# Row means from summed weight columns, so that centring starts before the last product

## The chip, the cores and the metric

The kernel runs on one core of a Trainium2 chip. The metric is device time in microseconds (us) for one execution. All times below come from one profiled execution or from the timed runs of the kernel before.

## The reference, cut to what matters

One decoder layer: a projection of `x` (256 rows of 1024), two attention branches, gates, an output projection and a layer norm over the 1024 columns of a row. Only the end is touched:

```python
merged = gate_a * ya + gate_b * yb
out = jnp.einsum('bsd,de->bse', merged, w_out[l])
x = layer_norm(DN_ALPHA * x + out, ln_gamma[l], ln_beta[l])

def layer_norm(x, g, b):
    mu = jnp.mean(xf, axis=-1, keepdims=True)
    var = jnp.mean(jnp.square(xf - mu), axis=-1, keepdims=True)
    return (xf - mu) * lax.rsqrt(var + LN_EPS) * g + b
```

## The kernel before

Each float32 weight tile (`wraw`, 128x1024) is loaded on the SP queue, rounded on ScalarE to `wh` and its remainder is formed on VectorE as `wl`, so that three products (`mh*wh`, `ml*wh`, `mh*wl`) stand for one float32 product. `fetch` issues the load and the rounding, `split` the remainder; both run several tiles ahead of TensorE. The order of instructions on each engine is the order in which the code is written.

The end of the program is a loop over two blocks of 128 rows (`t`). For each block, `products` multiplies the eight 128-deep slices of the merged activations (`mm`, its halves `mh` and `ml`) by the eight tiles of `w_out`, 24 products for each group of columns. Block 0 runs all 1024 columns at once in two PSUM banks of tag `acc`. Block 1 runs three groups one after the other: columns 0 to 512, 512 to 768 (the third quarter) and 768 to 1024 (the last quarter), in banks of tag `sc`. After each group VectorE adds the residual (line 373) and takes the statistics of each quarter (line 375, `bn_stats`).

When the last quarter of a block has its statistics, line 383 joins them to mean and variance, ScalarE takes the root (385) and the norm is applied in three pieces. Columns 0 to 416 and 416 to 832 get two VectorE passes each: `centre` (390: subtract the mean, times gamma) and 404 (times 1/deviation, plus beta), then a store on the SP queue. Columns 832 to 1024 go over ScalarE (398: scale and `shift`, a small VectorE result of line 397), then two GpSimd passes (399: times gamma, 400: plus beta) and a store on the ACT queue (406). Block 0's norm runs beside block 1's products; nothing runs beside block 1's.

Of the kernel before, what the change touches and what calls it, by code (L numbers as in the profile page):

```python
# [11 lines left out]
F32 = mybir.dt.float32  # L12
F32R = mybir.dt.float32r
# [4 lines left out]
P = 128  # L18
# [18 lines left out]

WARM = 9
RAWS = 5


@with_exitstack
def hybrid_layer(ctx: ExitStack, tc: tile.TileContext, xT, x2, w_t, w_v, w_a, w_b, w_o,
# [56 lines left out]
    order += [("o", k) for k in range(NK)]  # L100
    ahead = {"v": 2, "t": 3, "a": 4, "b": 5, "o": 7}
    raws, ready = {}, {}

    def fetch(kind, n):
# [12 lines left out]
        src = {"v": lambda: w_v[:, n, :], "t": lambda: w_t[n], "a": lambda: w_a[n], "b": lambda: w_b[n],  # L117
               "o": lambda: w_o[n * P:(n + 1) * P, :]}[kind]()
        raw = wp.tile([P, 1024], F32, tag="raw", name="wraw", bufs=RAWS)
        wh = wp.tile([P, 1024], F32R, tag="wh", name="wh", bufs=8)  # L120
        parts = 2 if (kind, n) == ("v", 0) else 1
        cuts = [slice(i * width // parts, (i + 1) * width // parts) for i in range(parts)]
        for cut in cuts:
            nc.sync.dma_start(raw[:, cut], src[:, cut])
        for cut in cuts:
            nc.scalar.activation(wh[:, cut], raw[:, cut], AF.Copy)  # L126
        raws[kind, n] = raw, wh, width

    def split(kind, n):
# [6 lines left out]
        wl = wp.tile([P, 1024], F32R, tag="wl", name="wl", bufs=8)  # L136
        nc.vector.tensor_sub(wl[:, :width], raw[:, :width], wh[:, :width].bitcast(F32))  # L137
        ready[kind, n] = wh, wl

    cursors = [0, 0]  # L140
# [216 lines left out]
    nc.sync.dma_start(gb[:, 1, :], beta.to_broadcast([P, D]))  # L357
    sd = work.tile([P, 1], F32, name="sd")
    nc.scalar.activation(sd, eps, AF.Sqrt)
    for t in range(2):  # L360
        ts = slice(t * P, (t + 1) * P)
        res = work.tile([P, D], F32, tag="res", name="res")
        st = work.tile([P, 4, 6], F32, name="st")

        def products(cuts):
            accs = [bank("acc" if t == 0 else "sc" if i < 2 else "pt")[:, :b - a] for i, (a, b) in enumerate(cuts)]
            for k in range(NK):
                wh, wl = weights("o", k)
                for a, w, s0, s1 in ((mh, wh, k == 0, False), (ml, wh, False, False), (mh, wl, False, k == NK - 1)):
                    for acc, (lo, hi) in zip(accs, cuts):  # L370
                        nc.tensor.matmul(acc, a[:, k, ts], w[:, lo:hi], start=s0, stop=s1)  # L371
            for acc, (lo, hi) in zip(accs, cuts):
                nc.vector.scalar_tensor_tensor(res[:, lo:hi], xr[:, t, lo:hi], ALPHA, acc, op0=ALU.mult, op1=ALU.add)
                for q in range(lo // S, hi // S):
                    nc.vector.bn_stats(st[:, q, :], res[:, q * S:(q + 1) * S])

        if t == 0:
            products([(0, 512), (512, 1024)])
        else:
            for cut in ((0, 512), (512, 768), (768, 1024)):  # L380
                products([cut])
        mv = work.tile([P, 2], F32, name="mv")
        nc.vector.bn_aggr(mv, st)  # L383
        sd = work.tile([P, 1], F32, name="sd")
        nc.scalar.activation(sd, mv[:, 1:2], AF.Sqrt, bias=eps)  # L385
        cuts = [slice(0, 416), slice(416, 832)]
        last = slice(832, D)

        def centre(cut):
            nc.vector.scalar_tensor_tensor(res[:, cut], res[:, cut], mv[:, 0:1], gb[:, 0, cut],  # L390
                                           op0=ALU.subtract, op1=ALU.mult)

        centre(cuts[0])
        rstd = work.tile([P, 1], F32, name="rstd")
# [6 lines left out]
        for cut in cuts:  # L401
# [76 lines left out]
```

## Time and profile before

| | us |
|---|---|
| median of 3 timed runs | 203.61 (203.3 to 203.8) |
| the profiled execution | 203.97 |
| its span, first to last instruction | 202.2 |
| the difference, outside the span | 1.77 |
| TensorE busy | 192.9 of 202.2 |
| VectorE busy | 134.2 |
| ScalarE busy | 113.2 |
| GpSimd busy | 17.1 |

The span is what the trace shows; the device time has 1.77 us more in this execution. "Busy" counts the time in which an instruction of the engine was under way. TensorE's granted clock had a mean of 0.994 of full speed.

### The profile page before, as it was taken

Reading aid. Unit: us, or ns where it says so; the run is one execution under the profiler, and the core shown is the slowest. Engines: PE = TensorE matmul, PEld = TensorE weight load, DVE = VectorE, ACT = ScalarE, POOL = GpSimd, SP = SyncE. Lnnn points to the kernel's source line nnn. Section 1 sums busy time; section 2 is a strip of 40 time slices with the busy share of each in tenths; the row PEclk is TensorE's granted clock in tenths of the full one; section 3 lists DMA queues with packets and bytes.
Section 4 is the critical chain, followed back from the end, with each engine's and each line's share of the span. In section 5 each row is a group of like instructions: output and inputs, shape, how many; then the busy total and the mean of one; then the engine's idle time right before and its main releaser. Section 6 shows DMA issues by size and latency. Waiting matters only on the chain.

```text
span 202.2 us, 3837 instructions
## 1 busy us (share of the span) xinstructions
PE 192.9 (95%) x1469; PEld 181.7 (90%) x1469; DVE 134.2 (66%) x268; ACT 113.2 (56%) x225; POOL 17.1 (8%) x29
## 2 busy tenths in 40 slices
PE   8899999999999999999999999999999999999940
PEld 3699999999998998989999999999999999888940
DVE  0595268999987874685777546446585867557753
ACT  4585648677985776775679444246554636620110
POOL 7070000110110100100000000000000000000303
PEclk9999999999999999999999999999999999999997
DMA  5999999947354233054667865474737499200202
GB/s 129 318 393 334 256 295 302 282 132 246 120 172 143 105 104 109 6 177 139 199 203 230 296 209 169 146 216 135 289 143 258 133 349 362 96 2 0 104 0 104
DMA packets 14081, 37.42 MB, mean 185 GB/s; under 512 B 1632, under 2 KB 5744, under 8 KB 14064
## 3 DMA queue, kind: packets, MB, share of 16 engines
q1 hardware_dynamic: 13520, 36.51, 55.8%
q0 software_dynamic: 256, 0.49, 0.7%
q8 instruction: 11, 0.18, 0.4%
q10 hardware_dynamic: 288, 0.20, 0.3%
q14 instruction: 6, 0.05, 0.1%
HBM read 35.75 MB, written 1.44 MB: 184 GB/s over the span
## 4 chain that ended last, share of the span: by engine, by line
PE 93%; DMA 2%; DVE 1%; ACT 1%; POOL 0%; POOLq 0%; SPq 0%; issue 0%
PE ps_acc L165 21%; PE ps_acc L166 21%; PE ps_acc L168 21%; PE ps_sc L371 6%; PE ps_acc L371 5%; PE ps_acc L277 4%; PE ps_sc L277 3%; PE ps_pt L242 3%; PE ps_o L259 2%; DMA wraw<-in_w_v 2%; PE ps_sc L205 1%; PE ps_sc L206 1%; PE ps_sc L207 1%; PE ps_o L261 1%; POOL res L399 0%; POOLq L474 0%
## 5 line engine op out<-in xcount | busy, mean ns | idle before, releaser
L137 DVE TENSOR_TENSOR wl<-wraw,wh 128x1024 fp32r<-128x1024 f32 (+1 forms) x61 | 70.2, 1167 | 7.8 <-ACT wh L126 7.5
L165 PE MATMUL ps_acc<-xh,wh 128*128 128x256 f32 x296 | 72.8, 284 | 0.0
L166 PE MATMUL ps_acc<-xl,wh 128*128 128x256 f32 x296 | 72.6, 283 | 0.0
L126 ACT ACTIVATE wh<-wraw 128x1024 fp32r<-128x1024 f32 (+2 forms) x62 | 60.8, 995 | 9.8 <-DMA wraw<-in_w_t 5.4
L165 PEld LDWEIGHTS ps_acc<-xh,wh 128*128 128x128 f32 x296 | 56.8, 192 | 0.5 <-issue 0.2
L166 PEld LDWEIGHTS ps_acc<-xl,wh 128*128 128x128 f32 x296 | 56.8, 192 | 0.3
L168 PE MATMUL ps_acc<-xh,wl 128*128 128x256 f32 x296 | 41.5, 283 | 0.0
L168 PEld LDWEIGHTS ps_acc<-xh,wl 128*128 128x128 f32 x296 | 38.2, 192 | 0.0
L339 ACT ACTIVATE sg<-ps_acc,bg 128x256 f32<-128x256 f32 x16 | 7.6, 475 | 20.9 <-PE ps_acc L168 20.9
L166 PE MATMUL ps_acc<-yl,wh 128*128 128x256 f32 x64 | 16.1, 283 | 0.0
L165 PE MATMUL ps_acc<-yh,wh 128*128 128x256 f32 x64 | 16.1, 283 | 0.0
L344 DVE TENSOR_TENSOR ga<-ps_acc,sg 128x256 f32<-128x256 f32 x8 | 3.4, 423 | 14.7 <-ACT wh L126 14.7
L165 PEld LDWEIGHTS ps_acc<-yh,wh 128*128 128x128 f32 x64 | 12.3, 192 | 0.0
L166 PEld LDWEIGHTS ps_acc<-yl,wh 128*128 128x128 f32 x64 | 12.3, 192 | 0.0
L399 POOL TENSOR_TENSOR res<-res,gb 128x192 f32<-128x192 f32 x2 | 1.8, 916 | 109.9 <-ACT res L398 109.9
L371 PE MATMUL ps_sc<-wh,mm 128*128 128x256 f32 (+1 forms) x48 | 10.7, 318 | 0.0
L168 PE MATMUL ps_acc<-yh,wl 128*128 128x256 f32 x64 | 10.3, 283 | 0.0
L349 ACT ACTIVATE mm<-m 128x256 fp32r<-128x256 f32 x8 | 3.3, 417 | 11.4 <-DVE m L348 11.4
L385 ACT ACTIVATE sd<-mv,eps 128x1 f32<-128x1 f32 x2 | 0.6, 294 | 16.1 <-DVE mv L383 16.1
L168 PEld LDWEIGHTS ps_acc<-yh,wl 128*128 128x128 f32 x64 | 8.8, 192 | 0.0
L371 PEld LDWEIGHTS ps_sc<-wh,mm 128*128 128x128 f32 x48 | 8.1, 191 | 0.7
L371 PE MATMUL ps_acc<-wh,mm 128*128 128x512 f32 x32 | 8.6, 390 | 0.0
(142 smaller groups left out, 269.0 us busy)
## 6 DMA issues: line engine op xcount, KB each, us to landing
wraw<-in_w_t SPq DMA_DIRECT2D x37, 512.0 KB, 3.7
wraw<-in_w_o SPq DMA_DIRECT2D x8, 512.0 KB, 4.6
wraw<-in_w_v SPq DMA_DIRECT2D x7, 320.0 KB, 5.1
toep<-rd SPq DMA_DIRECT2D x16, 128.0 KB, 7.3
wraw<-in_w_a SPq DMA_DIRECT2D x4, 512.0 KB, 3.8
wraw<-in_w_b SPq DMA_DIRECT2D x4, 512.0 KB, 4.3
xraw<-in_xT SPq DMA_DIRECT2D x8, 128.0 KB, 5.0
xr<-in_x SPq DMA_DIRECT2D x1, 1024.0 KB, 8.1
```

The lines of the kernel that those rows point to most:

```text
L126: nc.scalar.activation(wh[:, cut], raw[:, cut], AF.Copy)
L137: nc.vector.tensor_sub(wl[:, :width], raw[:, :width], wh[:, :width].bitcast(F32))
L165: nc.tensor.matmul(acc, wh[:, cols[k]], ah[:, a0 + k, :], start=(k == 0), stop=False)
L166: nc.tensor.matmul(acc, wh[:, cols[k]], al[:, a0 + k, :], start=False, stop=False)
L168: nc.tensor.matmul(acc, wl[:, cols[k]], ah[:, a0 + k, :], start=False, stop=(k == n - 1))
L242: nc.tensor.transpose(pt[:, b * P:(b + 1) * P], pr[:, j, b * P:(b + 1) * P], ident)
L259: nc.tensor.matmul(o[r, :], vv[:, 0, c], pts[:, :S], start=True, stop=False)
L277: nc.tensor.matmul(vacc[t][c], a[:, k, t * P:(t + 1) * P], w[:, c * 320:(c + 1) * 320], start=s0, stop=s1)
L339: nc.scalar.activation(sg, acc, AF.Sigmoid, bias=bg[:, at:at + 1])
L344: nc.vector.tensor_mul(ga[:, c, :], acc, sg)
L349: nc.scalar.activation(mh[:, c, :], m, AF.Copy)
L371: nc.tensor.matmul(acc, a[:, k, ts], w[:, lo:hi], start=s0, stop=s1)
```

## The change

The tiles `wh` and `wl` are laid out as four quarters of 258 columns (`OW`) in place of one stretch of 1024, so that each quarter has two spare columns. For the tiles of `w_out`, ScalarE and VectorE write through that layout, and VectorE also sums the last quarter of each weight tile over its columns into one column of `sums`. After block 0's products are issued, `place_sums` splits these sums into a rounded part and a remainder, and GpSimd copies them into the two spare columns of the third quarter: 16 copies of 128x2. In block 1 the third quarter's products run over 258 columns, so that column 256 of its bank holds what the last quarter's products will add up to along the row. With the statistics of three quarters and a sum of the residual's last quarter (`xs`) this gives minus the mean (`below`) one quarter earlier. Columns 0 to 768 of block 1 are centred and multiplied by gamma in the time of the last quarter's products. The pieces change too: columns 0 to 192 (`early`) now go over ScalarE and GpSimd, 192 to 640 and 640 to 1024 over VectorE.

```diff
-        wh = wp.tile([P, 1024], F32R, tag="wh", name="wh", bufs=8)
+        wh = wp.tile([P, 4 * OW], F32R, tag="wh", name="wh", bufs=8)
...
+            nc.vector.tensor_reduce(sums[:, n:n + 1], raw[:, 3 * S:], axis=mybir.AxisListType.X, op=ALU.add)
...
+    xs = work.tile([P, 1], F32, name="xs")
+    nc.vector.tensor_reduce(xs, xr[:, 1, 3 * S:], axis=mybir.AxisListType.X, op=ALU.add)
+    nc.vector.tensor_scalar_mul(xs, xs, -ALPHA / D)
+    def place_sums():
+        parts = [work.tile([P, NK], F32R, name=f"sums_{i}", bufs=1) for i in range(2)]
+        nc.scalar.activation(parts[0], sums, AF.Copy)
+        nc.vector.tensor_sub(parts[1], sums, parts[0].bitcast(F32))
+        for k in range(NK):
+            for w, part in zip(ready["o", k], parts):
+                nc.gpsimd.tensor_copy(w[:, 2 * OW + S:3 * OW], part[:, k:k + 1].to_broadcast([P, 2]))
...
+        def centre_early(below):
+            nc.scalar.activation(res[:, early], res[:, early], AF.Identity, bias=below)
+            nc.gpsimd.tensor_tensor(res[:, early], res[:, early], gb[:, 0, early], op=ALU.mult)
...
-            for cut in ((0, 512), (512, 768), (768, 1024)):
-                products([cut])
+            products([(bank("sc"), 0, 2, S)])
+            acc = bank("sc")[:, :OW]
+            products([(acc, 2, 1, OW)])
+            part = work.tile([P, 2], F32, name="part")
+            nc.vector.bn_aggr(part, st[:, :3, :])
+            nc.vector.scalar_tensor_tensor(below, acc[:, S:S + 1], -1.0 / D, xs, op0=ALU.mult, op1=ALU.add)
+            nc.vector.scalar_tensor_tensor(below, part[:, 0:1], -0.75, below, op0=ALU.mult, op1=ALU.add)
+            centre_early(below)
+            centre(slice(E, 3 * S), below)
+            products([(bank("pt")[:, :S], 3, 1, S)])
+            nc.vector.bn_aggr(mv, st)
+            nc.scalar.activation(sd, mv[:, 1:2], AF.Sqrt, bias=eps)
+            centre(slice(3 * S, D), below)
         nc.vector.reciprocal(rstd, sd)
-        shift = work.tile([P, 1], F32, name="shift")
-        nc.vector.scalar_tensor_tensor(shift, mv[:, 0:1], -1.0, rstd, op0=ALU.mult, op1=ALU.mult)
-        nc.scalar.activation(res[:, last], res[:, last], AF.Identity, bias=shift, scale=rstd)
-        nc.gpsimd.tensor_tensor(res[:, last], res[:, last], gb[:, 0, last], op=ALU.mult)
-        nc.gpsimd.tensor_tensor(res[:, last], res[:, last], gb[:, 1, last], op=ALU.add)
-        for cut in cuts:
-            if cut is not cuts[0]:
-                centre(cut)
+        nc.scalar.activation(res[:, early], res[:, early], AF.Copy, scale=rstd)
+        nc.gpsimd.tensor_tensor(res[:, early], res[:, early], gb[:, 1, early], op=ALU.add)
+        for cut in (slice(E, 640), slice(640, D)):
             nc.vector.scalar_tensor_tensor(res[:, cut], res[:, cut], rstd, gb[:, 1, cut], op0=ALU.mult, op1=ALU.add)
             nc.sync.dma_start(out[ts, cut], res[:, cut])
-        nc.scalar.dma_start(out[ts, last], res[:, last])
+        nc.scalar.dma_start(out[ts, early], res[:, early])
```

VectorE, the end of block 1, from the third quarter's residual on. Before:

```order
L373 SCALAR_TENSOR_TENSOR res<-xr,ps_sc 128x256
L375 BN_STATS st<-res 128x6
L373 SCALAR_TENSOR_TENSOR res<-xr,ps_sc 128x256
L375 BN_STATS st<-res 128x6
L383 BN_AGGR mv<-st 128x2
L390 SCALAR_TENSOR_TENSOR res<-res,mv,gb 128x416
L395 RECIPROCAL rstd<-sd 128x1
L397 SCALAR_TENSOR_TENSOR shift<-mv,rstd 128x1
L404 SCALAR_TENSOR_TENSOR res<-res,rstd,gb 128x416
L390 SCALAR_TENSOR_TENSOR res<-res,mv,gb 128x416
L404 SCALAR_TENSOR_TENSOR res<-res,rstd,gb 128x416
```

VectorE at the same place in the changed kernel, from the third quarter's statistics on:

```order
L406 BN_STATS st<-res 128x6
L433 BN_AGGR part<-st 128x2
L434 SCALAR_TENSOR_TENSOR below<-ps_sc,xs 128x1
L435 SCALAR_TENSOR_TENSOR below<-part,below 128x1
L409 SCALAR_TENSOR_TENSOR res<-res,below,gb 128x576
L404 SCALAR_TENSOR_TENSOR res<-xr,ps_pt 128x256
L406 BN_STATS st<-res 128x6
L439 BN_AGGR mv<-st 128x2
L409 SCALAR_TENSOR_TENSOR res<-res,below,gb 128x256
L442 RECIPROCAL rstd<-sd 128x1
L447 SCALAR_TENSOR_TENSOR res<-res,rstd,gb 128x448
L447 SCALAR_TENSOR_TENSOR res<-res,rstd,gb 128x384
```

Two centring passes of 416 behind the last quarter became one of 576 ahead of it and one of 256 behind it; `shift` is gone.

GpSimd, from its last instruction of the attention part (`pr_`, line 232) to the end. Before:

```order
L232 TENSOR_TENSOR pr__1102<-pr__1102,rs_1132 128x2x128
L399 TENSOR_TENSOR res_2278<-res_2278,gb_2273 128x192
L400 TENSOR_TENSOR res_2278<-res_2278,gb_2273 128x192
L399 TENSOR_TENSOR res_2374<-res_2374,gb_2273 128x192
L400 TENSOR_TENSOR res_2374<-res_2374,gb_2273 128x192
```

GpSimd in the changed kernel from the second of its 16 copies, of which the rest alternate between `wh` and `wl` for one slice after the other:

```order
L387 COPY wl_2117<-sums_1_2367 128x2
L387 COPY wh_2114<-sums_0_2366 128x2
L387 COPY wl_2169<-sums_1_2367 128x2
...
L387 COPY wl_2321<-sums_1_2367 128x2
L413 TENSOR_TENSOR res_2286<-res_2286,gb_2278 128x192
L445 TENSOR_TENSOR res_2286<-res_2286,gb_2278 128x192
L413 TENSOR_TENSOR res_2406<-res_2406,gb_2278 128x192
L445 TENSOR_TENSOR res_2406<-res_2406,gb_2278 128x192
```

The copies stand ahead of block 0's norm. In block 1 the first pass (413) no longer stands behind the last product.

TensorE, the passage from the first two quarters of block 1 (512 columns) to the third, with what an instruction waits for. Before, no product of the third quarter has a wait:

```order
L371 MATMUL ps_sc_2376<-wl_2306,mm_1426 128x512
L371 MATMUL ps_sc_2404<-wh_2089,mm_1426 128x256 x2
L371 MATMUL ps_sc_2404<-wl_2116,mm_1426 128x256
L371 MATMUL ps_sc_2404<-wh_2113,mm_1426 128x256 x2
L371 MATMUL ps_sc_2404<-wl_2167,mm_1426 128x256
```

In the changed kernel:

```order
L399 MATMUL ps_sc_2412<-wl_2321,mm_1427 128x512
L399 MATMUL ps_sc_2440<-wh_2090,mm_1427 128x258 [waits Pool_49]
L399 MATMUL ps_sc_2440<-wh_2090,mm_1427 128x258
L399 MATMUL ps_sc_2440<-wl_2117,mm_1427 128x258 [waits Pool_49]
L399 MATMUL ps_sc_2440<-wh_2114,mm_1427 128x258 [waits Pool_49]
L399 MATMUL ps_sc_2440<-wh_2114,mm_1427 128x258
L399 MATMUL ps_sc_2440<-wl_2169,mm_1427 128x258 [waits Pool_49]
```

Every first use of a `wh` or `wl` tile in the third quarter now waits for a GpSimd copy, 16 waits in 24 products.

## Rows read from the trace of the kernel before

**Rows 1.** Chain that ended last, from the last product: start us, us, what.

```profile
194.59 0.43 DVE res L373
...
195.04 0.44 DVE st L375
...
195.50 0.28 DVE mv L383
...
195.80 0.65 DVE res L390
196.45 0.09 DVE rstd L395
...
196.56 0.17 DVE shift L397
...
196.75 0.56 ACT res L398
...
197.38 0.91 POOL res L399
...
198.33 0.85 POOLq L474
```

**Rows 2.** Timeline, end of block 1: start us, us, engine, line, operation.

```profile
195.86 0.29 ACT L385 ACTIVATE sd<-mv,eps 128x1 f32<-128x1 f32 x1 [8.00 <-DVE mv L383]
196.37 0.16 DVE L395 RECIPROCAL rstd<-sd 128x1 f32<-128x1 f32 x1
...
196.64 0.64 DVE L404 SCALAR_TENSOR_TENSOR res<-res,rstd,gb 128x416 f32<-128x416 f32 x1
...
197.20 0.65 DVE L390 SCALAR_TENSOR_TENSOR res<-res,mv,gb 128x416 f32<-128x416 f32 x1
...
197.88 0.86 DVE L404 SCALAR_TENSOR_TENSOR res<-res,rstd,gb 128x416 f32<-128x416 f32 x1
198.37 0.82 POOL L400 TENSOR_TENSOR res<-res,gb 128x192 f32<-128x192 f32 x1
199.22 0.34 ACTq L406 DMA_DIRECT2D out<-res  x1
```

**Rows 3.** Block 1's stores: issues on SP, then landing times of all three.

```profile
L405 SPq DMA_DIRECT2D out<-res x2: 332/332/333, 197.3 to 198.8; - x2
...
DMA to landing us min/median/max: 1.9/1.9/2.1
```

**Rows 4.** Timeline, block 1's last two quarters on TensorE and VectorE.

```profile
188.43 0.87 DVE L404 SCALAR_TENSOR_TENSOR res<-res,rstd,gb 128x416 f32<-128x416 f32 x1
188.64 0.40 PE L371 MATMUL ps_sc<-wh,mm 128*128 128x256 f32 x2
...
189.23 0.67 DVE L373 SCALAR_TENSOR_TENSOR res<-xr,ps_sc 128x512 f32<-128x512 f32 x1
...
191.51 0.40 PE L371 MATMUL ps_sc<-wh,mm 128*128 128x256 f32 x2
...
191.71 0.42 DVE L373 SCALAR_TENSOR_TENSOR res<-xr,ps_sc 128x256 f32<-128x256 f32 x1 [1.02 <-PE ps_sc L371]
...
194.27 0.28 PE L371 MATMUL ps_sc<-wl,mm 128*128 128x256 f32 x1
```

**Rows 5.** Groups by line and form: count, then busy us and mean ns.

```profile
L285 POOL TENSOR_SCALAR nsink<-sink 128x8 f32<-128x8 f32 x1 | 0.4, 402 | 0.0
...
L78 POOL MEMSET eps<- 128x1 f32 x1 | 0.1, 88 | 0.0
```

**Rows 6.** Timeline, block 0: VectorE's last remainders, TensorE's last two products.

```profile
174.27 1.22 DVE L137 TENSOR_TENSOR wl<-wraw,wh 128x1024 fp32r<-128x1024 f32 x1
176.39 3.50 DVE L137 TENSOR_TENSOR wl<-wraw,wh 128x1024 fp32r<-128x1024 f32 x3 [0.90 <-ACT wh L126]
...
182.74 0.61 PE L371 MATMUL ps_acc<-wl,mm 128*128 128x512 f32 x2
...
183.17 0.69 DVE L373 SCALAR_TENSOR_TENSOR res<-xr,ps_acc 128x512 f32<-128x512 f32 x1 [3.28 <-PE ps_acc L371]
```

More of the change, by code (lines that the diff above doesn't have):

```diff
@@ L39 @@
 RAWS = 5
+OW = 258
+E = 192
 @with_exitstack
@@ L102, in hybrid_layer, with quarters @@
     raws, ready = {}, {}
+    sums = const.tile([P, NK], F32, name="sums")
+    def quarters(w):
+        return w.rearrange("p (a b) -> p a b", a=4)[:, :, :S]
     def fetch(kind, n):
@@ L124, in fetch @@
             nc.sync.dma_start(raw[:, cut], src[:, cut])
-        for cut in cuts:
-            nc.scalar.activation(wh[:, cut], raw[:, cut], AF.Copy)
+        if kind == "o":
+            nc.scalar.activation(quarters(wh), raw.rearrange("p (a b) -> p a b", a=4), AF.Copy)
+        else:
+            for cut in cuts:
+                nc.scalar.activation(wh[:, cut], raw[:, cut], AF.Copy)
         raws[kind, n] = raw, wh, width
@@ L135, in split @@
         raw, wh, width = raws.pop((kind, n))
-        wl = wp.tile([P, 1024], F32R, tag="wl", name="wl", bufs=8)
-        nc.vector.tensor_sub(wl[:, :width], raw[:, :width], wh[:, :width].bitcast(F32))
+        wl = wp.tile([P, 4 * OW], F32R, tag="wl", name="wl", bufs=8)
+        if kind == "o":
+            nc.vector.tensor_sub(quarters(wl), raw.rearrange("p (a b) -> p a b", a=4), quarters(wh).bitcast(F32))
+            nc.vector.tensor_reduce(sums[:, n:n + 1], raw[:, 3 * S:], axis=mybir.AxisListType.X, op=ALU.add)
+        else:
+            nc.vector.tensor_sub(wl[:, :width], raw[:, :width], wh[:, :width].bitcast(F32))
         ready[kind, n] = wh, wl
@@ L363, in hybrid_layer, with products @@
         st = work.tile([P, 4, 6], F32, name="st")
-        def products(cuts):
-            accs = [bank("acc" if t == 0 else "sc" if i < 2 else "pt")[:, :b - a] for i, (a, b) in enumerate(cuts)]
+        def products(accs):
             for k in range(NK):
-                wh, wl = weights("o", k)
+                wh, wl = (w.rearrange("p (a b) -> p a b", a=4) for w in weights("o", k))
                 for a, w, s0, s1 in ((mh, wh, k == 0, False), (ml, wh, False, False), (mh, wl, False, k == NK - 1)):
[L370 to L375, printed above, removed]
@@ L377, in hybrid_layer @@
-        if t == 0:
-            products([(0, 512), (512, 1024)])
-        else:
-            for cut in ((0, 512), (512, 768), (768, 1024)):
-                products([cut])
[L382 to L391, printed above, removed]
@@ L393, in hybrid_layer @@
-        centre(cuts[0])
-        rstd = work.tile([P, 1], F32, name="rstd")
-        nc.vector.reciprocal(rstd, sd)
-        shift = work.tile([P, 1], F32, name="shift")
-        nc.vector.scalar_tensor_tensor(shift, mv[:, 0:1], -1.0, rstd, op0=ALU.mult, op1=ALU.mult)
-        nc.scalar.activation(res[:, last], res[:, last], AF.Identity, bias=shift, scale=rstd)
-        nc.gpsimd.tensor_tensor(res[:, last], res[:, last], gb[:, 0, last], op=ALU.mult)
-        nc.gpsimd.tensor_tensor(res[:, last], res[:, last], gb[:, 1, last], op=ALU.add)
@@ L401, in hybrid_layer @@
-        for cut in cuts:
-            if cut is not cuts[0]:
-                centre(cut)
+                    for acc, q, n, cols in accs:
+                        nc.tensor.matmul(acc, a[:, k, ts], w[:, q:q + n, :cols], start=s0, stop=s1)
+            if t == 0:
+                place_sums()
+            for acc, q, n, _ in accs:
+                cut = slice(q * S, (q + n) * S)
+                nc.vector.scalar_tensor_tensor(res[:, cut], xr[:, t, cut], ALPHA, acc[:, :n * S], op0=ALU.mult, op1=ALU.add)
+                for i in range(q, q + n):
+                    nc.vector.bn_stats(st[:, i, :], res[:, i * S:(i + 1) * S])
@@ new lines, in centre @@
+        def centre(cut, below):
+            nc.vector.scalar_tensor_tensor(res[:, cut], res[:, cut], below, gb[:, 0, cut], op0=ALU.add, op1=ALU.mult)
+        def centre_early(below):
+            nc.scalar.activation(res[:, early], res[:, early], AF.Identity, bias=below)
+            nc.gpsimd.tensor_tensor(res[:, early], res[:, early], gb[:, 0, early], op=ALU.mult)
+        early = slice(0, E)
+        mv = work.tile([P, 2], F32, name="mv")
+        below = work.tile([P, 1], F32, name="below")
@@ new lines, in hybrid_layer @@
+        sd = work.tile([P, 1], F32, name="sd")
+        rstd = work.tile([P, 1], F32, name="rstd")
+        if t == 0:
+            products([(bank("acc"), 0, 2, S), (bank("acc"), 2, 2, S)])
+            nc.vector.bn_aggr(mv, st)
+            nc.scalar.activation(sd, mv[:, 1:2], AF.Sqrt, bias=eps)
+            nc.vector.tensor_scalar_mul(below, mv[:, 0:1], -1.0)
+            centre_early(below)
+            centre(slice(E, D), below)
+        else:
+            products([(bank("sc"), 0, 2, S)])
[5 more added lines that the diff above has]
+            nc.vector.scalar_tensor_tensor(below, part[:, 0:1], -0.75, below, op0=ALU.mult, op1=ALU.add)
+            centre_early(below)
+            centre(slice(E, 3 * S), below)
+            products([(bank("pt")[:, :S], 3, 1, S)])
+            nc.vector.bn_aggr(mv, st)
+            nc.scalar.activation(sd, mv[:, 1:2], AF.Sqrt, bias=eps)
+            centre(slice(3 * S, D), below)
```

## The prediction

> **What bounds the kernel now.** I read the page first: TensorE is busy for 192.9 of 202.2 us, so a change elsewhere can only pay where TensorE is idle, at the very end. The chain of waits shows that end [rows 1]: behind the last product come, one after the other, the residual on VectorE at 194.59, the statistics, mean and variance, a centring pass, the reciprocal, `shift`, ScalarE's pass, and two GpSimd passes. The timeline gives the last act, the store issued on the ACT queue at 199.22 [rows 2]. From 194.59 to there are 4.63 us, and nothing of it runs beside products. From that issue to the span's end are 202.2 - 199.22 = 2.98 us, of which a store's landing takes 1.9 to 2.1 us [rows 3]; the change does not touch them.
>
> The other branch of the tail is nearly as long: VectorE's second pass over columns 416 to 832 runs from 197.88 for 0.86 us [rows 2], so its store goes to SP at 198.76 (198.8 in [rows 3]). With 2.1 us to land that is 200.86; the ACT store lands at 199.22 + 1.9 = 201.12. Both have to get shorter.
>
> One more thing is to be seen there. The same pass of line 404 takes 0.64 us at 196.64 and 0.86 us at 197.88 [rows 2], and 0.87 us in block 0 [rows 4]. The ends explain it: GpSimd's pass of line 399 starts at 197.38, inside the VectorE pass of line 390 that ends at 197.85, and ends 0.44 us after that, at 198.29 [rows 1, 2]. Line 404's pass, begun at 197.88, ends 0.45 us after this, at 198.74. GpSimd's line 400, begun at 198.37, ends at 199.19, again 0.45 us later. I read this as taking turns: a VectorE pass with `res` and `gb` as inputs and a GpSimd pass do not overlap, and the work proper of 192 columns on GpSimd is about 0.45 us. The Trainium skill, SBUF — State Buffer, section "Who interferes with whom", says that a VectorE instruction with two SBUF inputs and a GpSimd instruction that reads SBUF exclude each other for the whole instruction; the trace agrees with these 0.45 us. Without this rule the sum below would be the 1.38 us of its upper bound in place of 1.13.
>
> **The change, part by part.**
>
> *The tail of block 1.* Up to mean and variance nothing changes: from the residual's start to 195.80 are 1.21 us [rows 1]. Then:
>
> - Centring shrinks from 416 columns (0.65 us [rows 1]) to 256. VectorE's residual takes 0.42 us for 256 columns and 0.67 for 512 [rows 4], so about 1 ns a column; 160 columns less give 0.49 us, to 196.29. The reciprocal began 0.08 us before the end of the pass ahead of it (196.37 against 196.45 [rows 1, 2]); so it begins at 196.21, which is later than the root on ScalarE at 195.86 + 0.29 = 196.15 [rows 2]. It ends at 196.37, and what waits for it starts at 196.40.
> - `shift` is gone; ScalarE's pass starts at 196.40 in place of 196.75. I leave it at 0.56 us [rows 1], with 0.07 us to hand over: GpSimd may start at 197.03.
> - GpSimd's gamma pass, 0.91 us [rows 1], is no longer there. What is left is the beta pass.
> - VectorE makes two passes in place of three: 448 columns from 196.40, 0.64 + 32 ns = 0.68 us, to 197.08; then 384 columns, begun 0.08 us before that end as in rows 2 (197.20 against 197.28), about 0.61 us, to 197.61. Its store goes to SP at 197.64, 1.12 us earlier than 198.76.
> - GpSimd's beta pass meets these two. By the turns above it comes behind the second one: 197.61 + 0.45 = 198.06, and the ACT store 0.03 us later at 198.09. That is 1.13 us earlier than 199.22. If GpSimd gets its turn between the two, it ends at 197.53 and the second VectorE pass at about 197.95: the SP store is then last, 0.8 us earlier than before, and with 2.1 us it lands at 200.08 against 201.12, a gain of 1.04. I take 1.13, as the second pass waits for nothing in front of it.
>
> The bounds of this term: if GpSimd is not held up at all, it ends at 197.48, and the SP store decides, landing at 199.74: 1.38 us gained. If the beta pass takes its whole old row of 0.82 us [rows 2] behind the second VectorE pass, the ACT store goes out at 198.46: 0.76 us gained.
>
> *The last quarter as cover.* The moved work has to fit between the third quarter's residual at 191.71 and the last quarter's at 194.59 [rows 4], 2.88 us. On VectorE: residual 0.42, statistics 0.44 and `bn_aggr` 0.28 [rows 1], the two small instructions 0.17 each like `shift` [rows 1], a centring pass of 576 columns (0.65 + 160 ns = 0.81), and some 0.1 us between them: 2.39 us, so it is done at 194.10. One of the small ones reads PSUM, which no row shows at that size; with the 0.42 us of a 256-column residual for it the end is 194.35. Beside it ScalarE (0.56) and GpSimd (0.45 behind VectorE's pass) are done with the early columns by about 194.5. So it costs nothing; without that cover each part would be paid in full.
>
> *The sums of the weights.* Eight sums of 256 columns on VectorE, and one of the residual. No row shows a sum; the nearest is the statistics' pass over 256 columns, 0.44 us [rows 1], and I take that; above I would go to a remainder pass of 1024 columns, 1.22 us, below to 0.16 (a reciprocal) [rows 2, 6]. Where it matters is block 0, whose products need the last remainder at 182.74 [rows 6]. Before, VectorE began the last four remainders at 174.27. Now 0.6 us of residual sum stand ahead, then four times 1.22 and three sums: 174.27 + 0.6 + 4.88 + 1.32 = 181.07, still 1.7 us early. A sum would have to take about 0.85 us to stall TensorE; at 1.22 the stall is some 1.5 us. The loads of the last three tiles reuse buffers that the sums read, so they go out one or two sums later, 0.4 to 0.9 us; the remainders that need them, at 176.39 and after [rows 6], have the same 1.7 us to spare. Behind the last remainder VectorE waited from 179.89 to 183.17 [rows 6], which covers the eighth sum and the split.
>
> *The 16 copies on GpSimd.* They begin when the sums are split, by about 182.0 (181.07, a sum of 0.44, then a small ScalarE and a small VectorE step), and the k-th pair is needed at 188.64 + 0.36 k, as eight slices take 191.51 - 188.64 us [rows 4]. A copy of two columns lies between the memset of one column, 0.09 us, and a pass over 8 columns, 0.40 us [rows 5]. I take 0.40: 16 make 6.4 us, to 188.4. Block 0's VectorE passes lie in that time, 832, 448 and 384 columns from about 186.5, and by the turns above a copy waits for the 832-column pass (1.06 us) and may wait for the next ones; that moves the last copy to about 190.3, needed at 191.3. Nothing is lost. The 16 waits themselves I charge with nothing, since the copies are done before TensorE comes to them; the nearest row is the 0.03 us from GpSimd's end at 199.19 to the ACT store [rows 2], and 16 of those, 0.5 us, are the upper bound.
>
> *Products of 258 columns.* Two columns more in 24 products, at 0.36 us for 3 x 256 columns [rows 4] less than 0.5 ns a column: 0.02 us. Block 0's own norm has three passes on VectorE in place of four, so the residual of the first two quarters at 189.23 [rows 4] is not later.
>
> **Sum.** 1.13 - 0.02, rounded: 1.1 us. The profiled execution of 203.97 us (span 202.2 and 1.77 around it) becomes 202.85. The median of 203.61 lies 0.36 below that execution, so I forecast 202.5 us. 0.3% of it is 0.6 us, about what a measurement here can tell from no change.
>
> **The rivals.**
>
> - *Slower: the third quarter waits for GpSimd.* Place: the first product of each `wh` and `wl` in block 1's third quarter. 16 copies from 182.0 reach their need when one takes (191.3 - 182.0) / 16 = 0.58 us with no hold-up. If a copy costs as much as GpSimd's 192-column pass, 0.82 us [rows 2], the last is ready at 195.1, TensorE is 3.8 us late and the time is 203.6 - 1.1 + 3.8 = 206.3. For: two-column copies are not in the trace, and they take turns with block 0's passes. Against: 8 columns took 0.40 us, and one column 0.09. The change loses once a copy takes more than (191.3 + 1.1 - 182.0) / 16 = 0.65 us. Chance 0.08, of which 0.02 lie within 0.3%.
> - *No change: the new layout slows products everywhere.* All weight tiles now have rows of 4 x 258 columns, and 1469 products read them or run beside them. 0.75 ns for each would eat 1.1 us: 203.6. No row has such a layout; nothing speaks for it but that it was not tried. Chance 0.10: 0.07 within 0.3%, 0.03 slower.
> - *Less than forecast: the tail's stores and passes collide.* Three stores go out within 1.0 us (197.1, 197.6, 198.1) where they took 1.9 (197.3 to 199.2 [rows 3]). If the last lands 0.3 us later and the beta pass takes 0.82 us, 0.4 to 0.5 us are left: 203.2. Against it: in all three landings the time was 1.9 to 2.1 us. Chance 0.08, 0.06 of it within 0.3%.
>
> **Chances and range.** The forecast has 0.74, with a range of its own of 202.2 to 202.9 by the bounds 1.38 and 0.76. Faster: 0.74 + 0.02 = 0.76. Same: 0.02 + 0.07 + 0.06 = 0.15. Slower: 0.09. The range of 202.0 to 203.4 takes in the forecast with the spread of the runs, the collision and part of the no-change case.
>
> **What would show it.** Right: the last residual still starts near 194.6, the last centring pass has 256 columns and about 0.49 us, no GpSimd gamma pass stands behind it, and the ACT store goes out near 198.1. VectorE's pass of 576 columns ends before 194.4. The copies end before 190.5 and TensorE has no idle time between 172 and 194. Wrong: idle time of TensorE that ends by GpSimd in the third quarter; products of 256 columns more than 0.12 us apart; the last quarter's residual starting behind the 576-column pass and not behind TensorE; a GpSimd beta pass that ends later than 198.5.

## The result and the profile after

The changed kernel takes 200.94 us (median of 4 runs, 200.81 to 201.19) where the kernel before takes 203.54 beside it: ratio 0.986 (95%: 0.981 to 0.990), 2.6 us less. The forecast was 202.5 us in a range of 202.0 to 203.4. So the sign was right, and the gain is more than twice the 1.1 us that were worked out. In two more groups of runs the changed kernel came to 0.987 (0.983 to 0.991) and 0.989 (0.984 to 0.994).

The page of its profiled execution (200.9 us), span and first part:

```profile
span 199.1 us, 3871 instructions
...
PE 190.9 (96%) x1469; PEld 179.2 (90%) x1469; DVE 137.9 (69%) x280; ACT 114.5 (58%) x228; POOL 19.0 (10%) x45
```

TensorE is busy for 2.0 us less (192.9 before), with the same 1469 products. No step of the prediction has that. The chain that ended last in the changed kernel, from the last projection tile on (start us, us, what):

```profile
167.46 0.94 PE ps_acc L183 x8
...
169.80 11.22 PE ps_acc L399 x48
181.03 8.48 PE ps_sc L399 x48
189.51 2.88 PE ps_pt L399 x24
192.41 0.43 DVE res L404
192.87 0.44 DVE st L406
193.33 0.28 DVE mv L439
193.69 0.30 ACT sd L440
194.01 0.18 DVE rstd L442
194.21 0.69 DVE res L447
194.90 0.91 DVEq L517
```

The same view of the kernel before, at the last projection tile:

```profile
170.05 0.96 PE ps_acc L168 x8
...
172.45 10.91 PE ps_acc L371 x48
```

Eight products of 256 columns take 0.94 us in place of 0.96, and the 48 products of 512 columns 11.22 in place of 10.91. The last residual starts at 192.41 in place of 194.59 [rows 1]: 2.2 us are won before the tail begins. The first projection product and the first of the seventh projection tile, in the timeline of before and then of after:

```profile
21.16 0.28 PE L165 MATMUL ps_acc<-xh,wh 128*128 128x256 f32 x1
...
42.34 0.28 PE L165 MATMUL ps_acc<-xh,wh 128*128 128x256 f32 x1
```

```profile
20.31 0.28 PE L180 MATMUL ps_acc<-xh,wh 128*128 128x256 f32 x1
...
41.69 0.27 PE L180 MATMUL ps_acc<-xh,wh 128*128 128x256 f32 x1
```

These points, the start of the chain's row of 48 output products and that of the last residual cut the span into stretches, in us (the span is given to 0.1 us, and so the tail is good to about 0.05):

| | to the first projection product | first six tiles | seventh tile to output products | output products to last residual | tail |
|---|---|---|---|---|---|
| before | 21.16 | 21.18 | 130.11 | 22.14 | 7.61 |
| after | 20.31 | 21.38 | 128.11 | 22.61 | 6.69 |
| after, 2nd profile | 22.84 | 20.71 | 128.11 | 22.61 | 6.73 |
| after, 3rd profile | 20.34 | 21.03 | 128.12 | 22.61 | 6.70 |

Only the first two columns differ between executions of one kernel; they hold the first loads. The others repeat to 0.04 us and give -2.00 + 0.47 - 0.92 = -2.45 us. The tail was forecast (-1.13); the other two terms were not.

It is not the clock. The stretch from 20 to 172 us, of after and of before (the columns behind POOL are granted clock, DMA share, GB/s):

```profile
20.00:172.00 152.00, 151.78 (x1255) 146.26 (x1254) 108.09 (x223) 95.99 (x197) 5.68 (x8) 1.00 0.62 200
```

```profile
20.00:172.00 152.00, 152.00 (x1248) 147.28 (x1247) 105.27 (x215) 94.92 (x196) 5.67 (x8) 1.00 0.62 198
```

The granted clock is 1.00 (2.4 GHz) in both, and TensorE has next to no idle time in either. The products themselves stand closer. Before, they start 119.5 to 120.0 ns apart in every tile, pauses left out. After, each tile has a pace of its own. Two tiles of the changed kernel (the 12th and the 20th projection tile), in the chain:

```profile
65.95 0.94 PE ps_acc L183 x8
...
98.39 0.91 PE ps_acc L183 x8
```

Over their whole tiles these are 117.8 and 114.0 ns a product, in the same weight buffer.

**The tail.** Timeline of the changed kernel, block 1, from the last centring pass:

```profile
193.51 0.42 DVE L409 SCALAR_TENSOR_TENSOR res<-res,below,gb 128x256 f32<-128x256 f32 x1
...
194.21 1.59 DVE L447 SCALAR_TENSOR_TENSOR res<-res,rstd,gb 128x448 f32<-128x448 f32 x2
...
194.81 0.59 POOL L445 TENSOR_TENSOR res<-res,gb 128x192 f32<-128x192 f32 x1 [2.59 <-ACT res L444]
194.93 1.24 SPq L448 DMA_DIRECT2D out<-res  x2
195.43 0.34 ACTq L449 DMA_DIRECT2D out<-res  x1
```

GpSimd's beta pass took its turn between VectorE's two passes: the second ends at 195.80, and its store on SP is the last. The prediction had this case beside the one it chose, with a gain of 1.04.

**The cover and the copies.** The small pass that reads PSUM, the third quarter's centring and the next residual in the timeline, then the first and the last copy:

```profile
190.62 0.10 DVE L434 SCALAR_TENSOR_TENSOR below<-ps_sc,xs 128x1 f32<-128x1 f32 x1
...
190.94 0.82 DVE L409 SCALAR_TENSOR_TENSOR res<-res,below,gb 128x576 f32<-128x576 f32 x1
...
192.41 0.42 DVE L404 SCALAR_TENSOR_TENSOR res<-xr,ps_pt 128x256 f32<-128x256 f32 x1 [0.65 <-PE ps_pt L399]
```

```profile
178.54 0.19 POOL L387 CAST wh<-sums 128x2 fp32r<-128x2 f32 x1 [93.83 <-ACT sums L383]
...
180.50 0.19 POOL L387 CAST wl<-sums 128x2 fp32r<-128x2 f32 x1
```

VectorE is done 0.65 us before the last quarter's products are. The 16 copies end at 180.69; the third quarter's products start about 186.6 (189.51 - 2.88). The sums, in the groups by line:

```profile
L150 DVE TENSOR_REDUCE sums<-wraw 128x1 f32<-128x256 f32 x8 | 3.3, 414 | 0.0
```

### The profile page after: what moved, and what is told of

Its sections match the earlier page's. It is cut to its first block, busy times and chain, and to the rows that moved or that the text cites. A ratio compares the mean times of both kernels' runs of the same rounds, so it can differ in the third digit from the quotient of the medians.

```text
span 199.1 us, 3871 instructions
## 1 busy us (share of the span) xinstructions
PE 190.9 (96%) x1469; PEld 179.2 (90%) x1469; DVE 137.9 (69%) x280; ACT 114.5 (58%) x228; POOL 19.0 (10%) x45
## 4 chain that ended last, share of the span: by engine, by line
PE 77%; DMA 9%; SPq 4%; DVE 3%; ACT 2%; issue 1%; DVEq 0%; ACTq 0%
PE ps_acc L180 19%; PE ps_acc L181 19%; PE ps_acc L183 19%; PE ps_acc L399 6%; PE ps_sc L399 4%; DMA wraw<-in_w_t 4%; PE ps_pt L257 3%; DMA rd<-rvec 3%; DMA wraw<-in_w_v 3%; PE ps_o L274 2%; SPq L119 2%; SPq L132 1%; PE ps_pt L399 1%; PE ps_sc L220 1%; ACT wh L137 1%; PE ps_sc L221 1%
## 5 line engine op out<-in xcount | busy, mean ns | idle before, releaser
L180 PE MATMUL ps_acc<-xh,wh 128*128 128x256 f32 x296 | 71.6, 281 | 0.0
L181 PE MATMUL ps_acc<-xl,wh 128*128 128x256 f32 x296 | 71.3, 280 | 0.0
L152 DVE TENSOR_TENSOR wl<-wraw,wh 128x1024 fp32r<-128x1024 f32 (+1 forms) x53 | 60.7, 1161 | 5.7 <-ACT wh L137 5.4
L137 ACT ACTIVATE wh<-wraw 128x1024 fp32r<-128x1024 f32 (+2 forms) x54 | 52.8, 991 | 8.6 <-DMA wraw<-in_w_t 5.2
L180 PEld LDWEIGHTS ps_acc<-xh,wh 128*128 128x128 f32 x296 | 55.8, 189 | 0.5 <-issue 0.2
L181 PEld LDWEIGHTS ps_acc<-xl,wh 128*128 128x128 f32 x296 | 55.7, 188 | 0.4
L387 POOL CAST wh<-sums 128x2 fp32r<-128x2 f32 x8 | 1.5, 187 | 93.8 <-ACT sums L383 93.8
L149 DVE TENSOR_TENSOR wl<-wraw,wh 128x1024 fp32r<-128x1024 f32 x8 | 9.8, 1220 | 0.1
L134 ACT ACTIVATE wh<-wraw 128x1024 fp32r<-128x1024 f32 x8 | 8.2, 1049 | 0.0
L399 PE MATMUL ps_sc<-wh,mm 128*128 128x512 f32 (+1 forms) x32 | 7.9, 339 | 0.0
```

Of the source, the lines that this page charges most:

```text
L134: nc.scalar.activation(quarters(wh), raw.rearrange("p (a b) -> p a b", a=4), AF.Copy)
L149: nc.vector.tensor_sub(quarters(wl), raw.rearrange("p (a b) -> p a b", a=4), quarters(wh).bitcast(F32))
L180: nc.tensor.matmul(acc, wh[:, cols[k]], ah[:, a0 + k, :], start=(k == 0), stop=False)
L181: nc.tensor.matmul(acc, wh[:, cols[k]], al[:, a0 + k, :], start=False, stop=False)
L399: nc.tensor.matmul(acc, a[:, k, ts], w[:, q:q + n, :cols], start=s0, stop=s1)
```

## The experiments

In the kernel before all rows of tiles between `xl` and the weights are multiples of 256 bytes, so every weight tile lies at one and the same offset from `xh`, modulo 256 bytes: 0. The change moves this twice: `sums` puts 32 bytes in between, and rows of 1032 columns are 4128 bytes, so that each further buffer lies 32 bytes on. Theory A: this offset sets the pace. Rivals: B, the gain is in the tail alone; C, a chance of the first loads.

**Layout alone, and tail alone.** `layout_only`:

```diff
+    pad = const.tile([P, NK], F32, name="pad")
...
-        wh = wp.tile([P, 1024], F32R, tag="wh", name="wh", bufs=8)
+        wh = wp.tile([P, 4 * OW], F32R, tag="wh", name="wh", bufs=8)
...
```

> The kernel before, with the weight tiles `wh` and `wl` as rows of 4 x 258 columns of which the first 1024 are used as one stretch, and a tile of 32 bytes a partition at the place of `sums`; its tail is untouched. Theory A (the pace of TensorE's 256-column products hangs on where a weight tile lies against the activations it meets): each weight buffer has its own pace, as in the changed kernel (113 to 120 ns a product, mean about 117.6, in place of 120.0 for all), and with 1080 such products the time falls by 1.6 to 2.6 us, to 201.0 to 201.9 us. Theory B (all of the gain is in the tail): no change, 203.5 us, and 120.0 ns for every product. Theory C (a chance of the first loads): no change in the pace; the first projection product may start elsewhere than 21.16 us.

`tail_alone`, from the changed kernel:

```diff
+ROW = 1088
...
-    sums = const.tile([P, NK], F32, name="sums")
+    sums = work.tile([P, NK], F32, name="sums", bufs=1)
...
-        wh = wp.tile([P, 4 * OW], F32R, tag="wh", name="wh", bufs=8)
+        wh = wp.tile([P, ROW], F32R, tag="wh", name="wh", bufs=8)
...
```

> The changed kernel with its weight tiles in rows of 1088 columns in place of 1032 (the quarters of 258 stay), and `sums` moved behind the weight tiles, so that every weight tile lies against the activations as before, modulo 256 bytes. The new tail, the sums, the copies and the 258-column products are all there. Theory A: the pace of the 256-column products is back at 120.0 ns, and only the tail's 0.92 us less the 0.3 us that the two-piece products of 512 columns cost remain: 202.6 to 203.0 us. Theory B: as the changed kernel, 200.9 us.

Measured: layout_only 201.94 us, ratio 0.990 (0.986 to 0.994); tail_alone 203.3, ratio 0.998 (0.995 to 1.0005). The chain of layout_only at the 20th tile and the output products, then that of tail_alone at the last tile and the output products:

```profile
98.80 0.91 PE ps_acc L171 x8
...
170.21 11.14 PE ps_acc L374 x48
```

```profile
169.12 0.96 PE ps_acc L184 x8
...
171.52 11.20 PE ps_acc L400 x48
```

Stretches in us, as above:

| | seventh tile to output products | output products to last residual | tail |
|---|---|---|---|
| layout_only | 128.12 | 22.42 | 7.57 |
| tail_alone | 130.09 | 22.53 | 6.75 |

layout_only has the changed kernel's 128.11 and none of its sums, copies or tail; tail_alone has all of these and the 130.11 of before. B and C fall. The gain of the change as planned, without the faster pace, is about half a microsecond by the stretches (-0.02 + 0.39 - 0.86 = -0.49) and by the medians; the interval of the timed runs, which reaches 1.0005, does not tell it from nothing.

**Equal offsets.** An unused tile of 128 bytes ahead of the weights, and the same ahead of those of tail_alone (`tail_and_pace`):

```diff
+    gap = ctx.enter_context(tc.tile_pool(name="gap", bufs=1))
+    pad = gap.tile([P, 32], F32, name="pad")
...
```

> The kernel before with nothing but an unused tile of 128 bytes a partition between the activations and the weight tiles, so that all weight tiles lie 128 bytes higher against the activations, as the fourth weight buffer does in the changed kernel (modulo 256 bytes). Theory A: all 1080 products of 256 columns run at that buffer's 113.4 ns in place of 120.0, 7.1 us less: 196.4 us; less than that if the loads or another engine cannot keep up. Rival A2 (not the place counts but that neighbouring tiles stand at different offsets): 120.0 ns and 203.5 us. Theory B: 203.5 us.

> The kernel of the run before this one with an unused tile of 128 bytes ahead of the weight tiles. Theory A: new tail and 113.4 ns for each of 1080 products together, 203.5 - 7.1 - 0.6 = 195.8 us. Theory B: 200.9 us. Rival A2: 202.8 us.

shift128 gave 202.8 us, 0.995 (0.992 to 0.997), with 118.8 ns a product; tail_and_pace 201.8, 0.990 (0.985 to 0.994), also 118.7. Neither the 113.4 ns of A nor the 120.0 of its rivals. Four more sizes of that tile:

> The kernel before with an unused tile of 96 bytes a partition ahead of the weight tiles; nothing else. So far: 128 bytes gave 118.8 ns for a product of 256 columns in nearly every tile, where the one tile of the changed kernel at that offset often had 113.3. Theory A (the offset of the weight tile against the activations alone sets the pace): as the third weight buffer of the changed kernel at this offset, 116.7 ns in every tile, 1080 x 3.3 ns = 3.6 us less up to the output products, about +0.3 us in these: 200.2 us. Theory A3 (a tile's pace hangs on its offset and on the step in which the products before it left the two reads, so that equal offsets settle into one pattern that need not be the best): some pace between 113 and 120 ns, the same in nearly all tiles, 197 to 203.8 us, not to be told from the offset. Theory B: 203.8 us.

> The same with 64 bytes. Theory A: as the second weight buffer of the changed kernel, 119.5 to 120.0 ns, no change in time but for the 512-column products. Theory A3: one pace for nearly all tiles, anywhere from 113 to 120 ns.

> The same with 32 bytes. Theory A: as the first weight buffer of the changed kernel, 118.1 ns, 1080 x 1.9 = 2.0 us less, some 0.3 us of it lost in the 512-column products. Theory A3: one pace for nearly all tiles, anywhere from 113 to 120 ns.

> The same with 160 bytes. Theory A: as the fifth weight buffer of the changed kernel, 117.8 ns, 2.4 us less, some 0.3 us of it lost in the 512-column products. Theory A3: one pace for nearly all tiles, anywhere from 113 to 120 ns.

shift96: 202.08 us, 0.992 (0.989 to 0.995), 117.4 ns. One execution each of the others: 201.37 (117.8 ns), 202.24 (118.2 ns), 204.22 (120.0 ns). That looked like no order at all, until the addresses that the program gives the buffers were set against the order of use. I had taken the buffers as used in the order of their addresses. In fact the first eight projection tiles of the changed kernel lie at 32, 0, 224, 64, 192, 96, 128, 160 bytes. So the numbers that these expectations foresaw belong to other offsets. Matched rightly (mean spacing within a tile, ns, over tiles with no wait inside):

| offset, bytes | 0 | 32 | 64 | 96 | 128 | 160 | 192 | 224 |
|---|---|---|---|---|---|---|---|---|
| first 22 projection tiles of the changed kernel | 119.5 to 120.0 | 118.0 to 118.2 | 113.3 to 117.8 | 117.5 to 118.4 | 118.5 to 118.9 | 119.8 | 114.7 to 118.0 | 116.8 |
| all tiles alike | 120.0 | 118.2 | 117.8 | 117.4 | 118.8 | 120.0 | 117.8 (x_only) | not yet run |

The offset gives the pace to about 1 ns, but for 64 bytes, where there are two: 113.3 and 117.8 ns. The row leaves out the changed kernel's later tiles: 15 with x, at 113.5 to 119.7 ns, and those with y, at 116.6 to 119.1. That 256 bytes is the step after which paces repeat is borne out by the rows of 1088 columns (4352 bytes, 17 x 256): tail_alone runs at the 120.0 ns of before and tail_and_pace at the pace of shift128, whose rows have 4096 bytes. The faster pattern ran on into the tile behind it (the 21st, at 192 bytes: 114.7 in place of 118.0).

**Which two things are at an offset.** `x_only`:

```diff
+    gap0 = const.tile([P, 16], F32, name="gap0")
...
     xh = const.tile([P, NK, S], F32R, name="xh")
     xl = const.tile([P, NK, S], F32R, name="xl")
+    gap1 = const.tile([P, 48], F32, name="gap1")
...
```

> The kernel before with the activations `xh` and `xl` alone moved by 64 bytes (an unused tile of 64 bytes ahead of them and one of 192 behind, so that `yh`, `yl`, `mm`, the weight tiles and the work tiles keep their offsets to each other, modulo 256 bytes). Theory D (it is the offset between the two operands that TensorE reads at a time): only the 888 products with `xh` and `xl` change their pace from 120.0 ns; those with `yh` and `yl` stay at 120.0 ns and the output products of 512 columns at 226.7 ns. Rival E (it is the offset between the weight tiles and what ScalarE, VectorE or the loads write beside them): nothing changes, all at 120.0 and 226.7 ns.

201.83 us in one execution. Its chain: four products with `yh`, eight with `xh`, the output products:

```profile
165.55 0.48 PE ps_acc L172 x4
...
167.92 0.94 PE ps_acc L172 x8
...
170.31 10.91 PE ps_acc L375 x48
```

Products with x run at 117.8 ns, all tiles with y but the first stay at 120.2 and the output products at 10.91 us. So it is TensorE's two operands against each other, the one that is loaded as weights (PEld) and the one that streams; where other engines write beside them does not set this pace. The Trainium skill, SBUF — State Buffer, section "Who interferes with whom", gives TensorE two independent read ports, one for each of these, and says that it never waits on anyone. As to other engines x_only agrees; against the two reads being independent speak the 113.3 to 120.0 ns, which hang on how the operands lie to each other.

**A forecast from the table, and the two patterns at 64.** `shift224` is the same unused tile with 224 bytes. `entry64` takes the new tail with single-stretch weight tiles of 1088 columns, whose data begin some columns in:

```diff
+    def lead_in(kind, n):
+        return 0 if kind == "o" else 56 if (kind, n) == ("t", 18) else 16
...
-        wh = wp.tile([P, 4 * OW], F32R, tag="wh", name="wh", bufs=8)
+        wh = wp.tile([P, ROW], F32R, tag="wh", name="wh", bufs=8)[:, lead_in(kind, n):]
...
+            nc.vector.tensor_reduce(sums[:, n:n + 1], raw[:, 2 * S:3 * S], axis=mybir.AxisListType.X, op=ALU.add)
...
+                nc.gpsimd.tensor_copy(w[:, D:D + 2], part[:, k:k + 1].to_broadcast([P, 2]))
...
+            products([(acc, 3, 1, S + 2)])
...
+            products([(bank("pt")[:, :S], 2, 1, S)])
```

The fourth quarter now comes third, with the summed columns right behind it.

> The kernel before with nothing but an unused tile of 224 bytes a partition ahead of the weight tiles. Theory A (the offset sets the pace; the buffers of the changed kernel now matched to their tiles by the program's allocation): 116.8 ns for products with x and y alike, from the seventh projection tile to the first output product 129.95 - 3.4 = 126.5 us. Theory A3 (a pattern of its own, not to be told from the changed kernel's tiles): some pace between 113 and 120 ns, as likely elsewhere as at 116.8.

> The new tail with single-stretch weight tiles, the weights of the projections 64 bytes into their tiles, but those of the 19th projection tile 224 bytes in; the output weights at 0. In the changed kernel the tile that followed such a pair ran at 113.3 ns, in shift64 nearly all tiles at 117.8. Theory of the pattern handed on: from the 20th tile on products run at 113.3 ns, as no wait stands between the tiles there; 117.8 before. The stretch from the seventh tile to the output products is then some 125.6 us in place of 127.9 in shift64. Rival (the pattern is a matter of the tile itself): 117.8 ns after as before.

shift224: 200.93 us in one execution, 116.7 ns in nearly every tile; the seventh tile to the output products 127.29 us, 2.8 less than before (3.4 foreseen). Its chain:

```profile
166.76 0.93 PE ps_acc L171 x8
...
169.09 11.19 PE ps_acc L374 x48
```

entry64: 196.46 us. Its chain:

```profile
163.57 0.91 PE ps_acc L183 x8
...
165.84 10.90 PE ps_acc L399 x48
```

The chain of shift64 at the last tile, with the same offset and 117.8 ns, and then that of all64, which follows below:

```profile
167.16 0.94 PE ps_acc L171 x8
```

```profile
163.76 0.91 PE ps_acc L183 x8
```

In entry64 all products from the 20th tile to the end of the projections run at 113.3 ns, and already from the 8th to the 15th. Was it the one tile at 224 bytes? `all64` leaves that out (`lead_in` returns 0 or 16), and entry64 was timed beside it:

> entry64 without its one tile at 224 bytes: all weights of the projections stand 64 bytes into their tiles. If the tile at 224 bytes brings the faster pattern in: 117.8 ns from the 19th tile on as in shift64, and 2.6 us more than entry64 (about 199 us). If the pattern stands from the eighth tile on and is handed over by whatever runs between (in entry64 the eighth to the fifteenth tile and the end of the eighteenth were at 113.3 ns already): 113.3 ns to the end, as entry64.

> The same kernel as entry64, timed. If its pattern is one of the program (all runs of one kernel so far kept their paces from profile to profile): 0.966 of the kernel before, 196.5 us. If it came by chance into that one execution: some runs near 199 us, and a profile with 117.8 ns in some stretch.

all64 took 196.67 us in one execution, at 113.3 ns from the 7th tile on but for three tiles with waits in them: the tile at 224 bytes was not needed. entry64_timed: 197.12 us (196.31 to 198.72), ratio 0.968 (0.964 to 0.971). In its profile the faster pattern set in at the 10th tile, not the 8th as in the first profile of the same kernel. So entry64's forecast came true in part by luck, as the tile from which it was worked out need not be there. The offset says which paces there are; what decides at 64 bytes between 113.3 and 117.8 is not shown. From the 20th tile on the faster pattern held to the end in all three profiles. shift64, whose operands stand at the same offset, had it too, in the 4th, the 16th and the 17th tile (113.5 to 113.8 ns, pauses left out), and was back at 117.8 in the 5th and the 18th. Why is open; its weight rows have 4096 bytes and those of entry64 and all64 4352, and no run changes that alone at this offset.

**Versions with one stable pace.** The layout of entry64 with another offset: `packed96` with an unused tile of 96 bytes ahead and only the output weights moved, 40 columns into their tiles; `packed224` without such a tile. The lines that place the weights, in packed96 (against the changed kernel) and in packed224 (against entry64):

```diff
+LEAD = 40
...
+    pad = gap.tile([P, 24], F32, name="pad")
...
+    def place(w, n=D):
+        return w[:, LEAD:LEAD + n]
...
```

```diff
-        return 0 if kind == "o" else 56 if (kind, n) == ("t", 18) else 16
+        return 0 if kind == "o" else 56
```

Each ran beside the changed kernel:

> The new tail with another layout of the weights: the weight tiles are single stretches again; all lie 96 bytes higher against the activations; for the output products they are written 40 columns into the tile, which brings them back to the offset of before against `mm`; the two summed columns stand behind the fourth quarter, which now comes third and carries the sums of the quarter that comes last. By the runs so far: first projection product to first output product 148.5 us as in shift96 (151.1 before), output products to last residual 22.3 as before (226.7 ns for 512 columns), the tail 6.7 (7.6 before): 3.5 us less than before, ratio 0.983, and 0.6 to 0.9 us less than the changed kernel. Rival (the offset of the output products costs nothing, the two-piece reading does): the same here, as both are undone.

> The changed kernel as it is, for a comparison on one chip with the run after this one. All theories: 0.98 to 0.99 of the kernel before, with the pace of its products as in its first profile, tile for tile (mean 117.6 ns).

> The kernel packed96 with 224 in place of 96 bytes: no unused tile, the weights of the projections stand 56 columns into their tiles, the output weights at 0. Theory A: 116.8 ns, the seventh projection tile to the first output product 126.5 us (127.95 in the changed kernel, 127.7 in packed96), the output products 22.3, the tail 6.3 to 6.7; together 2.2 us less than the changed kernel from the seventh tile on, ratio to the kernel before 0.976. Theory A3: between 0.97 and 0.99.

> The changed kernel as it is, for a comparison on one chip with the run after this one. All theories: 0.985 of the kernel before.

packed96: 200.43 us, 0.984 (0.980 to 0.988), beside 200.97 and 0.987 (0.983 to 0.991) for the changed kernel; the intervals overlap. packed224: 199.61, 0.980 (0.976 to 0.984), beside 201.02 and 0.989 (0.984 to 0.994). Stretches in us:

| | seventh tile to output products | output products to last residual | tail |
|---|---|---|---|
| packed96 | 127.83 | 22.13 | 6.33 |
| packed224 | 127.25 | 22.12 | 6.70 |
| entry64 | 124.61 | 22.13 | 6.73 |

packed224 has 116.7 ns a product, as foreseen, but its first stretch gains only 0.86 us on the changed kernel (128.11 to 127.25) where 1.45 were foreseen (127.95 to 126.5), and its ratio is 0.980 in place of 0.976. The passes of packed96's tail take as long as those of the others; the 0.4 us that it has less stand behind the issue of its last store.

The output products are back at 22.1 us. In layout_only they took 22.42 though its 512 columns are one stretch, and about 22.5 in the runs shift32 to shift224, where nothing but the offset differs: there the offset alone costs 0.3 to 0.4 us. But tail_alone, whose weight tiles start at the offset of before, took 22.53 as well, 0.39 more than before: there it is the reading in quarters of 258 columns, in two pieces or because the later quarters begin 8, 16 and 24 bytes further on; no run tells these two apart. Together the two cost less than their sum: the changed kernel has both and took 22.61. The best version of all is entry64, 6.5 us below the kernel before.

**Who holds whom up in the tail.** `no_beta` is tail_alone without one line:

```diff
-        nc.gpsimd.tensor_tensor(res[:, early], res[:, early], gb[:, 1, early], op=ALU.add)
```

> The kernel of the run tail_alone without GpSimd's last pass (beta is not added to columns 0 to 192). In tail_alone this pass stood at 196.44 to 197.03 us and VectorE's second pass ended at 197.44, 1.59 us after the first began. Theory of the turns (the pass took its turn between VectorE's two and held the second back): VectorE's two passes take 0.68 + 0.61 = 1.29 us, its last store is issued 0.3 us earlier and the stretch from the last residual to the end falls from 6.73 to about 6.45 us. Rival (the second pass itself takes 0.9 us, or the second store's landing decides): 1.59 and 6.7 us stay.

202.58 us in one execution. VectorE's two passes in the timeline of tail_alone, then of no_beta:

```profile
195.85 1.59 DVE L448 SCALAR_TENSOR_TENSOR res<-res,rstd,gb 128x448 f32<-128x448 f32 x2
```

```profile
195.95 1.21 DVE L447 SCALAR_TENSOR_TENSOR res<-res,rstd,gb 128x448 f32<-128x448 f32 x2
```

1.21 in place of 1.59 us: the GpSimd pass costs the second VectorE pass 0.38 us, as the turns say. The tail falls from 6.75 to 6.59 only; the rest came back between the last store's issue and the end of the span (3.3 us in tail_alone, 3.6 here).

## Why the prediction was wrong

- **The step that failed** is *Products of 258 columns*, with the rival *No change: the new layout slows products everywhere*. The step charged the new layout with two columns in 24 products, 0.02 us. It did not ask what the layout does to the other products, which have the same columns as before, and the premise that a gain can only come where TensorE is idle took its 192.9 busy us as fixed; they fell to 190.9. The rival asked, but only for a loss ("0.75 ns for each would eat 1.1 us"), as no row had such a layout. What stood in its place: 2.00 us less from the seventh tile to the output products, as the rows of 4128 bytes and `sums` move the weight tiles against the activations (1.99 us of it in layout_only), and 0.47 us more in the output products, by the same offset and the reading in quarters. An unknown price was bounded on one side only; with a bound of 2 us on the other side, a size that only the result gave, the range would have begun near 200.5.
- **The sign** was right mostly by luck: of 2.6 us the planned part is about 0.5, and tail_alone, which has that part alone, came to 0.998 (0.995 to 1.0005), no clear gain.
- **The tail** (1.13) measured 0.92, and 0.86 in tail_alone. The mechanism was right: no `shift`, no GpSimd gamma pass, two VectorE passes. The turn came out as in the case that was not chosen (1.04), and the last store was issued 3.43 us behind the start of the last residual in place of 4.63 [rows 1, 2]: 194.93 + 1.24, less 0.33 for an issue, is 195.84, and 195.84 - 192.41 = 3.43. That is 1.20 us earlier, and 0.3 of it was lost between that issue and the end, a stretch that the prediction took as untouched. The stores did not collide: they landed after 1.9 to 2.0 us (1.9 to 2.1 before), so the 0.3 us stand behind the last landing; what makes them is open, as the 0.4 us less of packed96 are. The centring pass took 0.42 us (0.49 forecast).
- **The last quarter as cover** was right: done at 191.76 with 0.65 us to spare; the small pass that reads PSUM took 0.10 us, below both its bounds.
- **The sums** took 0.41 us each (0.44 forecast). **The copies** took 0.19 us (0.40 forecast) and started 0.12 us apart at 178.54, so the rival in which the third quarter waits for them was far off.
- Not asked at all was how much single executions differ in their first stretch, in which the first loads arrive: the first projection product starts at 20.3 to 22.8 us in three profiles of the changed kernel. The medians level that out; a comparison of two spans does not.

## What to carry to other kernels

A change to a tile's row length or to what stands ahead of it moves every tile behind, and with it the pace of instructions that the diff does not touch: before trusting a gain, compare the spacing of unchanged instructions in both traces. Where a bound is unknown, bound it on both sides. And once a layout effect shows, undo it alone and do it alone: here the planned part was worth 0.5 us and the side effect 2; with the offset chosen on purpose, the whole came to 6.5.

## What the runs showed of the hardware

- Products of 256 columns (128x128 weights, float32r) start 113.3 to 120.0 ns apart at a granted clock of 1.00, by the offset of the weight tile against the streamed one modulo 256 bytes. Offset 0, where tiles lie whose row lengths are all multiples of 256 bytes, is with 160 the slowest for them; for products of 512 columns in one stretch (weights from `mm`) it is the fastest of the seven offsets run, 10.9 us for 48 against 11.14 to 11.24.
- At one offset more than one pattern can hold (64 bytes: 113.3 and 117.8 ns), and it can last over hundreds of products. That the two reads get in each other's way inside the memory is my reading; the runs show only that the pace hangs on the offset, and that one kernel entered the faster pattern at the 8th tile in one execution and at the 10th in another.
- GpSimd casts of 128x2 took 0.19 us each and started 0.12 us apart.
